# The low half of q and the second copy of k: written by the engines instead of by transfers

## The chip, the cores and the metric

One Trainium2 chip, one core. The time is that of one execution of the whole program on the device, in microseconds (us). The kernel before took 744.98 us, the median of 3 runs (744.69 to 747.67).

## The reference

One layer of a decoder on a sequence of 512 tokens with 1024 channels, in float32:

```
mod = silu(c) @ ada_w + ada_b          # shift1, scale1, gate1, shift2, scale2, gate2
h = rmsnorm(x) * (1 + scale1) + shift1
qa, ka, va, qb, kb, vb, ga, gb = split(h @ w_in)
ya = swa_attention(qa, ka, va) @ w_branch_a     # 8 query heads, 2 key heads, window of 128, sinks
yb = moba_attention(qb, kb, vb) @ w_branch_b    # 8 heads, blocks of 256
x = x + gate1 * ((sigmoid(ga) * ya + sigmoid(gb) * yb) @ w_out)
h2 = rmsnorm(x) * (1 + scale2) + shift2
x = x + gate2 * (relu(h2 @ w_mlp_in)^2 @ w_mlp_out)
out = rmsnorm(x)
```

A head is 64 wide, and the scores of both attentions are q times k with a bias by distance. With 512 tokens the second attention has two blocks, so that every query sees all earlier blocks.

## The kernel before

**Numbers in two parts.** A float32 value is held as a high part (rounded by ScalarE's copy into the matmul's type) and a low part (VectorE: value minus high part). `split(hi, lo, src)` at L69 to L72 does both: L71 on ScalarE, L72 on VectorE. A product of matrices is then three matmuls, high by high, low by high and high by low (`mm3`, L76 to L78).

**Scores.** A head has 64 channels, and the array takes 128 rows. So q is stacked: its high part on 64 partitions and its low part on the other 64. Tile `both[g]` is that stack for head g of a pair; head 0 has its high part on partitions 0 to 63, head 1 on 64 to 127. For k there are two tiles: `high[g]` has the high part on both halves, `low[g]` has the low part on one half and zeros on the other. A score then takes two matmuls of 128 rows, L440 in the loop of `Head.__init__`. The products q and k come out of the projection in PSUM, one bank (128 x 512) for a pair of heads: `g0p` and `pkv` for the windowed attention (tiles `qa`, `ka`), `pqk` for the other (tiles `qk`).

**The two functions that stack.** `stack_q` (L219 to L226) splits each half of the bank: high to its half of `both[g]`, low to a scratch tile `lo` at the same partitions, then a DMA on SyncE's queue takes `lo` to the other half (L225). `lo` has the tag `t`, a ring of three buffers that also gives `vaf` (L404), `ca*` and `cb*` (L483) and `sg*` (L573). `stack_k` (L228 to L235) splits into `high` and `low` and copies the high part to the other half by a DMA (L234). Callers: L401 and L406 (`qa0` to `qa3`), L403 (`ka`), L552 (`qk0` to `qk3`, q and k).

**Heads and dense work.** After the projections for the windowed attention (up to 58 us of the trace, with 0 to 58 in an order written by hand), `run` (L601) goes over 16 heads, 8 windowed (`a0`, `a4`, `a1`, ...) and 8 of the other attention (`b0` to `b7`). For each head in turn: scores (PSUM banks `sa*`, `sb*`; L440), on VectorE the bias and the row maximum (L441, into `pa*`, `pb*` and `ma*`, `mb*`), its negative (L444), on ScalarE the exponential (L445), the reciprocal of the sum (L451), the scaling (L456 on VectorE, L454 on ScalarE for block 3), transposes on TensorE (L470, banks `ta*`, `tb*`), a split of them (`pta*`, `ptb*`), the product with v (L481, banks `oa*`, `ob*`), a copy of the bank on ScalarE (L484, `ca*`, `cb*`) and one more matmul with a permutation, called swap here (L488), that adds the two halves; the result is split into `at0*`, `at1*`.

Between these steps `advance` takes steps of dense work from one list: the projection of v (`pv*`, weights `vw*` from the load `vbr*`, L511), of q and k (`pqk*`, weights `qkw*`), the gates (`pg*`, weights `gw*` from the load `gr*`, L566; sigmoid on ScalarE to `sg*`, L574), the branch products (`py*`, weights `bw*`), and the modulation for the second half (`ac2*`: ScalarE L154, VectorE L156, from the load `a`). The table `PACE` says how many steps stand at which place.

**What sets the order.** The program's order of every engine is fixed when the kernel is built. In the first stage and in the last ones it is written by hand; in between a scheduler places each engine's instructions by its own model of when operands and buffers are ready. Each engine then runs its list strictly in that order. PSUM has eight banks in one ring, and a bank that VectorE reads isn't read by ScalarE at the same time.

Of the kernel before, what the change touches and what calls it, by code (L numbers as in the profile page):

```python
# [10 lines left out]
F32 = mybir.dt.float32  # L11
F32R = mybir.dt.float32r
AF = mybir.ActivationFunctionType
ALU = mybir.AluOpType

P = 128
D = 1024
S = 512
# [19 lines left out]
def decoder_layer(ctx: ExitStack, tc: tile.TileContext, x, c, ada_w, ada_b, norm1_g, norm2_g, w_in,  # L38
# [3 lines left out]
    V, A, G, SY = nc.vector, nc.scalar, nc.gpsimd, nc.sync  # L42

    pz = ctx.enter_context(tc.tile_pool(name="pz", bufs=1, side="right"))
    p0 = ctx.enter_context(tc.tile_pool(name="p0", bufs=1))
# [23 lines left out]
    def split(hi, lo, src):  # L69

        A.activation(hi, src, AF.Copy)  # L71
        V.tensor_tensor(lo, src, hi.bitcast(F32), op=ALU.subtract)  # L72
# [38 lines left out]
    def slot(n, name, dt=F32):  # L111

        return p0.tile([P, 512], dt, name=name, tag=f"slot{n}")
# [96 lines left out]
    with ExitStack() as sa:  # L210
# [7 lines left out]

        def stack_q(name, src, both):  # L219

            lo = p0.tile([P, S], F32R, name=name + "l", tag="t", bufs=3)
            for g in range(2):
                r, o = slice(64 * g, 64 * g + 64), slice(64 - 64 * g, 128 - 64 * g)
                split(both[g][r], lo[r], src[r])
                SY.dma_start(both[g][o].bitcast(F32), lo[r].bitcast(F32))  # L225
            return both  # L226

        def stack_k(name, src, high, low):  # L228

            for g in range(2):  # L230
                r, o = slice(64 * g, 64 * g + 64), slice(64 - 64 * g, 128 - 64 * g)
                G.memset(low[g][o].bitcast(F32), 0.0)
                split(high[g][r], low[g][r], src[r])
                SY.dma_start(high[g][o].bitcast(F32), high[g][r].bitcast(F32))  # L234
            return high, low  # L235

        va = pa.tile([P, NT, 4, HD], F32R, name="va")
# [3 lines left out]
        with ExitStack() as ss:  # L241
# [152 lines left out]
            for s in range(2):  # L394
                w = wide(f"kvw{s}")
                split(w[0], w[1], kvr[:, :, s * P:(s + 1) * P])
                pkv.append(bank(f"pkv{s}"))
                for k in range(KT):
                    mm3(pkv[s], at(w, slice(None), k), at(hT, slice(None), k), first=k == 0, last=k == KT - 1)
                if s == 0:  # L400
                    qa = [stack_q("qa0", g0p[0], [qk_tile(f"qa0{g}") for g in range(2)])]  # L401
                    ka = [slot(n, f"ka{n}", F32R) for n in (4, 5, 6, 7)]
                    ka = stack_k("ka", pkv[0], ka[:2], ka[2:])  # L403
            vaf = scratch("vaf")  # L404
            A.activation(vaf, pkv[1], AF.Copy)
            qa += [stack_q(f"qa{j}", g0p[j], [qk_tile(f"qa{j}{g}") for g in range(2)]) for j in range(1, 4)]  # L406

        def turn_v():
# [126 lines left out]
        def proj_qk(i2):  # L535
            wr = []
            for s, col in ((0, C_QB), (1, C_KB)):
                t = raw(f"qkr{i2}{s}").rearrange("p (k n) -> p k n", k=KT)
                SY.dma_start(t, w0[:, :, col + i2 * 256:col + i2 * 256 + 256])
                wr.append(t)  # L540
            for half in range(2):
                i = 2 * i2 + half
                got, tiles = [], qk_tiles(f"qk{i}")
                for s in range(2):
                    w = cols_of(wr[s], half, f"qkw{i}{s}")
                    pb = bank(f"pqk{i}{s}")
                    for k in range(KT):
                        mm3(pb, at(w, slice(None), k), at(hT, slice(None), k), first=k == 0, last=k == KT - 1)
                        if k == 3:
                            yield  # L550
                    own = [[t[n] for t in tiles] for n in range(3)]
                    got.append(stack_q(f"qk{i}{s}", pb, own[0]) if s == 0 else stack_k(f"qk{i}{s}", pb, *own[1:]))  # L552
                    if s == 1:
                        qk[i] = got
                    yield
# [239 lines left out]
    for ci, (f0, f1) in enumerate(CHUNKS):  # L795
# [35 lines left out]
        else:  # L831
# [15 lines left out]
            for t in range(NT):  # L847
                o = [slot(4 + 2 * (t % 2) + h, f"o{t}{h}") for h in range(2)]
# [75 lines left out]
```

## Time and profile before

| | |
|---|---|
| median of 3 runs | 744.98 us |
| the profiled execution | 745.23 us |
| its span, first to last instruction | 743.5 us |
| mean granted clock of TensorE | 0.997 |
| busy TensorE, VectorE, ScalarE | 709.7, 459.1, 344.6 us |
| TensorE busy 58 to 240 us | 174.52 of 182 us |
| TensorE busy 300 to 700 us | 399.61 of 400 us |

TensorE works nearly all the time, so that what matters is where it stands still. The last two lines say that in the stage of the heads (58 to 240 us) it does so for 7.5 us, and in the long stage behind it hardly at all. Matmuls overlap in the profile: one of 128x512 is listed with 0.39 us while the next starts 0.23 us later, so that starts are read, not durations.

### The profile page before, as it was taken

How to read it: one execution, taken by the hardware profiler on the slowest of the kernel's cores; microseconds unless marked ns; L12 is line 12 of the kernel's file. 1: busy time of each engine (PE TensorE's matmuls, PEld its weight loads, DVE VectorE, ACT ScalarE, POOL GpSimd, SP SyncE). 2: the span in 40 equal slices, each digit the busy share in tenths (PEclk: the TensorE clock that was granted, in tenths of full speed). 3: DMA queues.
4: the chain of work that ended last, by engine and by line, in shares of the span. 5: the costliest groups of instructions: out<-in, count | busy, mean ns of one | idle time of the engine just before them, and what ended most of it. 6: DMA issues, size and time to landing. Idle time of an engine off the chain costs nothing.

```text
span 743.5 us, 9326 instructions
## 1 busy us (share of the span) xinstructions
PE 709.7 (95%) x3458; PEld 595.6 (80%) x3458; DVE 459.1 (62%) x959; ACT 344.6 (46%) x639; POOL 28.7 (4%) x40
## 2 busy tenths in 40 slices
PE   2799999998999999999999999999999999999996
PEld 1677889886887888888889888888888888888885
DVE  4874888887677867684478573252652527325765
ACT  3454787766786753343274442231332314322434
POOL 2220000000000000000120000000000000000001
PEclk9999999999999999999999999999999999999999
DMA  8994451566363864641415352233322332315103
GB/s 300 303 286 104 111 156 38 157 180 190 95 162 100 266 217 169 199 171 56 142 57 167 116 170 94 76 114 114 113 91 80 87 108 90 113 60 167 57 1 113
DMA packets 91146, 100.21 MB, mean 135 GB/s; under 512 B 3027, under 2 KB 70683, under 8 KB 91100
## 3 DMA queue, kind: packets, MB, share of 16 engines
q1 hardware_dynamic: 91100, 99.61, 43.6%
q8 instruction: 27, 0.44, 0.3%
q14 instruction: 19, 0.16, 0.1%
HBM read 94.03 MB, written 2.16 MB: 129 GB/s over the span
## 4 chain that ended last, share of the span: by engine, by line
PE 84%; ACT 4%; DMA 4%; DVE 3%; SPq 2%; issue 1%; POOL 0%; POOLq 0%; ACTq 0%; DVEq 0%
PE ph L77 8%; PE ph L76 8%; PE ph L78 8%; PE mo L78 7%; PE mo L76 7%; PE mo L77 7%; PE pg L76 3%; PE pg L78 3%; PE pg L77 3%; PE pqk L76 2%; PE py L78 2%; PE pqk L77 2%; PE py L76 2%; PE pqk L78 2%; PE py L77 2%
## 5 line engine op out<-in xcount | busy, mean ns | idle before, releaser
L800 ACT ACTIVATE r<-ph 128x512 f32<-128x512 f32 x32 | 18.8, 587 | 41.5 <-PE ph L78 26.8
L803 DVE TENSOR_TENSOR r<-r 128x512 f32<-128x512 f32 x32 | 21.9, 689 | 18.2 <-ACT a1h L802 8.0
L156 DVE SCALAR_TENSOR_TENSOR ac<-a,cs,ac 128x256 f32<-128x256 f32 x56 | 26.8, 479 | 3.5 <-ACT ac L154 2.9
L294 DVE SCALAR_TENSOR_TENSOR pac<-ad,cs,pac 128x256 f32<-128x256 f32 (+1 forms) x42 | 21.5, 523 | 9.8 <-ACT pac L292 9.4
L126 POOL TENSOR_TENSOR rstd<-rstd,mhalf 128x1 f32<-128x1 f32 x12 | 7.3, 610 | 373.3 <-DVE rstd L125 373.3
L711 DVE TENSOR_TENSOR rs<-mo,g2row 128x512 f32<-128x512 f32 x24 | 16.0, 686 | 9.1 <-PE mo L78 9.1
L445 ACT ACTIVATE pb<-pb,nb 128x128 f32<-128x128 f32 (+3 forms) x32 | 17.8, 557 | 8.1 <-DVE nb L444 7.7
L186 DVE SCALAR_TENSOR_TENSOR ma<-mw,cs,ma 128x512 f32<-128x512 f32 x28 | 21.0, 750 | 0.5
L76 PE MATMUL g0p<-hTh,g0h 128*128 128x512 f32 (+1 forms) x36 | 16.1, 448 | 3.8 <-ACT hTh L71 3.8
L445 ACT ACTIVATE pa<-pa,na 128x256 f32<-128x256 f32 (+1 forms) x32 | 15.2, 478 | 2.5 <-DVE na L444 2.4
L712 DVE TENSOR_TENSOR x_sb<-x_sb,rs 128x512 f32<-128x512 f32 x24 | 16.2, 685 | 0.0
L441 DVE CUSTOM_DVE_ANT_0 pa<-sa,ts,sink 128x256 f32<-128x256 f32 (+1 forms) x32 | 13.3, 445 | 3.8 <-PE sa L440 3.7
L441 DVE CUSTOM_DVE_ANT_0 pb<-sb,tm 128x128 f32<-128x128 f32 (+3 forms) x32 | 15.1, 488 | 0.2 <-PE sb L440 0.2
L77 PE MATMUL g0p<-hTl,g0h 128*128 128x512 f32 (+1 forms) x36 | 14.6, 406 | 0.0
L78 PE MATMUL g0p<-hTh,g0l 128*128 128x512 f32 (+1 forms) x36 | 14.4, 399 | 0.0
L440 PE MATMUL sb<-qk,qk 128*128 128x128 f32 (+3 forms) x64 | 12.8, 330 | 0.0
L76 PEld LDWEIGHTS g0p<-hTh,g0h 128*128 128x128 f32 x36 | 8.0, 222 | 5.1 <-ACT hTh L71 4.5
L282 POOL TENSOR_TENSOR g0l<-g0r,g0h 128x512 fp32r<-128x512 f32 x8 | 10.5, 1317 | 28.7 <-ACT g0h L281 24.4
L712 POOL TENSOR_TENSOR x_sb<-x_sb,rs 128x512 f32<-128x512 f32 x4 | 5.0, 1290 | 157.1 <-DVE rs L711 157.1
L440 PE MATMUL sa<-ka,qa 128*128 128x256 f32 (+1 forms) x64 | 10.9, 282 | 0.0
L470 PE MATMUL tb<-ident,pb 128*128 128x128 f32 x80 | 10.6, 274 | 0.3 <-DVE mb L441 0.3
L841 DVE TENSOR_TENSOR ml<-ml,g2row 128x512 f32<-128x512 f32 x8 | 5.1, 688 | 9.4 <-DMA ml<-in_w_mlp_out_dram 9.4
(1599 smaller groups left out, 2415.2 us busy)
## 6 DMA issues: line engine op xcount, KB each, us to landing
mi<-in_w_mlp_in_dram SPq DMA_DIRECT2D x16, 1024.0 KB, 6.3
mo<-in_w_mlp_out_dram SPq DMA_DIRECT2D x14, 1024.0 KB, 5.1
ad<-in_ada_w_dram SPq DMA_DIRECT2D x16, 512.0 KB, 7.9
a<-in_ada_w_dram SPq DMA_DIRECT2D x16, 512.0 KB, 5.3
gr<-in_w_in_dram SPq DMA_DIRECT2D x8, 1024.0 KB, 6.4
mw<-in_ada_w_dram SPq DMA_DIRECT2D x8, 1024.0 KB, 5.3
x_sb<-in_x_dram SPq DMA_DIRECT2D x8, 512.0 KB, 7.4
qkr<-in_w_in_dram SPq DMA_DIRECT2D x4, 1024.0 KB, 5.9
```

The lines of the kernel that those rows point to most:

```text
L76: nc.tensor.matmul(o, w[0], m[0], start=first, stop=False, **kw)
L77: nc.tensor.matmul(o, w[0], m[1], start=False, stop=False, **kw)
L78: nc.tensor.matmul(o, w[1], m[0], start=False, stop=last, **kw)
L156: V.scalar_tensor_tensor(acc, ad[:, k], cs[:, k:k + 1], acc, op0=ALU.mult, op1=ALU.add)
L186: V.scalar_tensor_tensor(acc, t[:, k], c1, acc, op0=ALU.mult, op1=ALU.add)
L294: V.scalar_tensor_tensor(part_ if k < KT - 1 else acc, ad(k), cs[:, k:k + 1], part_, op0=ALU.mult, op1=ALU.add)
L440: nc.tensor.matmul(pb[:, :w], q[g][:, i * P:e], k[n][g][:, e - w:e], start=n == 0, stop=n == 1)
L441: V.tensor_tensor_reduce(p[:, o:o + w], pb[:, :w], b[:, w - 1::-1] if w < b.shape[1] else b[:, ::-1], scale=SCALE, scalar=-3e38 if sk is N ...
L445: A.activation(p[:, o:o + w], p[:, o:o + w], AF.Exp, bias=neg[:, i:i + 1], accum_out=sums[:, i:i + 1])
L712: add.tensor_tensor(x_sb[:, t, cc], x_sb[:, t, cc], tm, op=ALU.add)
L800: A.activation(r, ph, AF.Relu)
L803: V.tensor_mul(r, r, r)
```

## The change

VectorE writes the low part of q straight to the other half of `both[g]`; the scratch tile `lo` and its DMA are gone. For k the second copy of the high part is made by ScalarE with one more copy out of PSUM, where a DMA took it from the first copy. 26 DMAs (16 of L225, 10 of L234) are no longer there, and 10 ScalarE instructions of 64x512 are new. From L226 on, the numbers of lines are lower by two in the kernel after.

```diff
         def stack_q(name, src, both):
 
-            lo = p0.tile([P, S], F32R, name=name + "l", tag="t", bufs=3)
             for g in range(2):
                 r, o = slice(64 * g, 64 * g + 64), slice(64 - 64 * g, 128 - 64 * g)
-                split(both[g][r], lo[r], src[r])
-                SY.dma_start(both[g][o].bitcast(F32), lo[r].bitcast(F32))
+                split(both[g][r], both[g][o], src[r])
             return both
 
         def stack_k(name, src, high, low):
...
                 G.memset(low[g][o].bitcast(F32), 0.0)
                 split(high[g][r], low[g][r], src[r])
-                SY.dma_start(high[g][o].bitcast(F32), high[g][r].bitcast(F32))
+                A.activation(high[g][o], src[r], AF.Copy)
             return high, low
```

The scheduler places the instructions of the stage of the heads anew. Up to 58 us and from about 245 us on the orders of all engines are the same as before. Three places follow; a name's last number is that of its buffer.

The first place is in front of head a0's scaling (near 81 us of the trace). VectorE before:

```order
L72 TENSOR_TENSOR qa3l_622<-g0p3_199,qa30_620 64x512
L441 ISA pa0_736,ma0_737<-sa02_752,ts0_734,sink_92 128x256
L441 ISA ma0_737 128x1
L72 TENSOR_TENSOR vw03l_773<-vbr0_641,vw03h_772 128x512
L444 TENSOR_SCALAR na0_739<-ma0_737 128x1 x2
L72 TENSOR_TENSOR va_91<-pva_727,va_91 128x4x128
L444 TENSOR_SCALAR na0_739<-ma0_737 128x1
L72 TENSOR_TENSOR qa3l_622<-g0p3_199,qa31_621 64x512
L441 ISA pa0_736,ma0_737<-sa03_758,ts0_734,sink_92 128x256
```

VectorE after:

```order
L72 TENSOR_TENSOR vw03l_761<-vbr0_629,vw03h_760 128x512
L439 ISA pa0_724,ma0_725<-sa01_734,ts0_722,sink_92 128x256
L439 ISA ma0_725 128x1
L442 TENSOR_SCALAR na0_727<-ma0_725 128x1
L439 ISA pa0_724,ma0_725<-sa02_740,ts0_722,sink_92 128x256
L439 ISA ma0_725 128x1
L72 TENSOR_TENSOR va_91<-pva_715,va_91 128x4x128
L439 ISA pa0_724,ma0_725<-sa03_746,ts0_722,sink_92 128x256
```

Both subtractions of `qa3` have moved ahead of these rows, and `vw03l` ahead of the scores `sa01` to `sa03`. ScalarE at the same place, before:

```order
L449 ACTIVATE ea0_764<-na0_739,sink_92 128x4
L71 ACTIVATE vb_634<-pv00_639 128x2x2x64
L445 ACTIVATE pa4_810,ua4_812<-pa4_810,na4_813 128x128
L445 ACTIVATE pa4_810,ua4_812<-pa4_810,na4_813 128x256 x2
L71 ACTIVATE vb_634<-pv01_640 128x2x2x64
L71 ACTIVATE vw10h_1305<-vbr1_1303 128x512
L71 ACTIVATE vw11h_1385<-vbr1_1303 128x512
L454 ACTIVATE pa0_736<-pa0_736,ua0_738 128x256
```

ScalarE after:

```order
L447 ACTIVATE ea0_752<-na0_727,sink_92 128x4
L443 ACTIVATE pa4_798,ua4_800<-pa4_798,na4_801 128x128
L71 ACTIVATE vw10h_1287<-vbr1_1285 128x512
L71 ACTIVATE vb_622<-pv00_627 128x2x2x64
L452 ACTIVATE pa0_724<-pa0_724,ua0_726 128x256
L71 ACTIVATE vb_622<-pv01_628 128x2x2x64
L71 ACTIVATE vw11h_1367<-vbr1_1285 128x512
```

`vw10h`, the high part of a weight of the load `vbr1`, has moved ahead of the copy to `vb` and, with fewer instructions between, stays ahead of head a0's scaling (L454, now L452).

The second place is at the scores of head a7 (near 137 us). VectorE before:

```order
L441 ISA pa7_1471,ma7_1472<-sa70_1475,ts7_1469,sink_92 128x128
L441 ISA ma7_1472 128x1
L156 SCALAR_TENSOR_TENSOR ac20_1593<-a20_1590,cs_86,ac20_1593 128x256
L444 TENSOR_SCALAR na7_1474<-ma7_1472 128x1
L441 ISA pa7_1471,ma7_1472<-sa71_1481,ts7_1469,sink_92 128x256
```

VectorE after:

```order
L439 ISA pa7_1453,ma7_1454<-sa71_1463,ts7_1451,sink_92 128x256
L439 ISA ma7_1454 128x1
L439 ISA pa7_1453,ma7_1454<-sa72_1469,ts7_1451,sink_92 128x256
L439 ISA ma7_1454 128x1
L442 TENSOR_SCALAR na7_1456<-ma7_1454 128x1
L72 TENSOR_TENSOR vb_622<-pv10_1283,vb_622 128x2x128
L439 ISA pa7_1453,ma7_1454<-sa73_1475,ts7_1451,sink_92 128x256
L439 ISA ma7_1454 128x1
L442 TENSOR_SCALAR na7_1456<-ma7_1454 128x1
L156 SCALAR_TENSOR_TENSOR ac20_1575<-a20_1572,cs_86,ac20_1575 128x256
```

The first step of `ac20` has moved from in front of the score `sa71` to behind the score `sa73`.

The third place is at the end of head b0 and the first gate (near 177 us). ScalarE before:

```order
L71 ACTIVATE gw02h_2136<-gr02_2134 128x1024
L71 ACTIVATE qk211_1571<-pqk21_1689 64x512
L71 ACTIVATE qk300_1735<-pqk30_1745 64x512
L71 ACTIVATE ptb10h_1994<-tb10_1993 128x512
L71 ACTIVATE ptb11h_2003<-tb11_2002 128x512
L484 ACTIVATE cb0_1904<-ob0_1895 128x512
L574 ACT_TABLE_LOAD
L574 ACTIVATE sg00_1987<-pg00_1912 128x512
```

ScalarE after:

```order
L482 ACTIVATE cb0_1880<-ob0_1871 128x512
L154 ACTIVATE ac22_1910<-a22_1907,cs_86 128x256
L443 ACTIVATE pb2_1915,ub2_1917<-pb2_1915,nb2_1918 128x128
L443 ACTIVATE pb2_1915,ub2_1917<-pb2_1915,nb2_1918 128x256
L71 ACTIVATE gw02h_2112<-gr02_2110 128x1024
L572 ACT_TABLE_LOAD
L572 ACTIVATE sg00_1963<-pg00_1888 128x512
L71 ACTIVATE at1h_625<-ob0_1871 64x512
L71 ACTIVATE qk211_1553<-pqk21_1668 64x512
L71 ACTIVATE qk300_1714<-pqk30_1724 64x512
L71 ACTIVATE ptb10h_1970<-tb10_1969 128x512
L71 ACTIVATE ptb11h_1979<-tb11_1978 128x512
```

`cb0` has moved ahead of `gw02h`, and the two `qk` copies and the two of `ptb1` from ahead of `sg00` to behind it. On TensorE the swap with `cb0` has moved ahead of the last score of head b2 and of b1's ten transposes.

## Rows read from the trace of the kernel before

**Rows 1.** The page's first part: busy time of each engine, share of the span and instructions.

```profile
PE 709.7 (95%) x3458; PEld 595.6 (80%) x3458; DVE 459.1 (62%) x959; ACT 344.6 (46%) x639; POOL 28.7 (4%) x40
```

**Rows 2.** The list of waits of TensorE (PE) between 55 and 240 us: waiting tile and line, released by; us in total, times, longest.

```profile
PE ob L488 <- ACT cb L484: 2.0, 1, 2.0
PE ob L481 <- ACT ptb40h L71: 1.7, 1, 1.7
PE pg L76 <- ACT sg L574: 1.4, 1, 1.4
PE ta L470 <- DVE pa L456: 1.2, 1, 1.2
...
PE pqk L76 <- DVE ma L441: 0.6, 1, 0.6
```

**Rows 3.** Busy time of each engine in stretches: stretch and its length, PE, PEld, DVE, ACT, POOL (instructions), granted clock, share of the DMA engines, GB/s.

```profile
58.00:240.00 182.00, 174.52 (x995) 151.81 (x994) 135.28 (x399) 128.33 (x277) 4.16 (x8) 0.99 0.49 132
80.00:90.00 10.00, 8.76 (x61) 7.83 (x60) 8.46 (x35) 9.14 (x28) 0.52 (x1) 1.00 0.61 160
180.00:190.00 10.00, 7.78 (x26) 6.10 (x27) 4.79 (x11) 6.99 (x13) 0.00 (x0) 0.83 0.63 154
230.00:240.00 10.00, 8.31 (x39) 6.62 (x38) 6.95 (x15) 8.78 (x17) 0.00 (x0) 1.00 0.28 71
300.00:700.00 400.00, 399.61 (x1824) 332.99 (x1824) 211.18 (x308) 140.79 (x223) 7.63 (x8) 1.00 0.35 113
```

**Rows 4.** The removed DMAs, from the views of lines L225 and L234: issue time in ns (min/median/max), first and last start; then the time to landing. The last line is of the waits of SyncE's queue between 58 and 250 us.

```profile
L225 SPq DMA_DIRECT2D qk<-qk30l x2: 467/1322/2176, 181.5 to 199.0; - x2
...
DMA to landing us min/median/max: 2.2/4.2/6.8
...
L234 SPq DMA_DIRECT2D qk<-qk x8: 461/467/511, 105.0 to 213.6; - x8
...
DMA to landing us min/median/max: 2.2/2.5/4.9
...
SPq L234 <- ACT qk L71: 20.4, 5, 6.8
```

**Rows 5.** Groups of ScalarE's (ACT) instructions between 58 and 240 us, by shape: count, busy us, mean ns, and the idle time just before them with its releaser.

```profile
L71 ACT ACTIVATE qk<-pqk 64x512 fp32r<-64x512 f32 x16 | 9.5, 591 | 1.0 <-PE sb L440 0.4 <-PE sa L440 0.3
...
L71 ACT ACTIVATE ka<-pkv 64x512 fp32r<-64x512 f32 x2 | 1.2, 584 | 1.5 <-DVE ka L72 1.5
```

**Rows 6.** VectorE (DVE) in order of time around the subtractions of `qa2`: start and duration in us. The first `qa2l` is on partitions 0 to 63, the second on 64 to 127.

```profile
75.89 0.68 DVE L72 TENSOR_TENSOR qa2l<-g0p,qa 64x512 fp32r<-64x512 f32 x1
76.50 0.67 DVE L72 TENSOR_TENSOR vw02l<-vbr,vw02h 128x512 fp32r<-128x512 f32 x1
77.23 0.69 DVE L72 TENSOR_TENSOR qa2l<-g0p,qa 64x512 fp32r<-64x512 f32 x1
77.96 0.35 DVE L441 CUSTOM_DVE_ANT_0 pa<-sa,ts,sink 128x128 f32<-128x128 f32 x1
```

**Rows 7.** Around head a0's transposes: TensorE and VectorE in order of time (start, duration, and in brackets the idle time before), then the landing of the two loads `vbr` of L511.

```profile
84.51 0.40 PE L440 MATMUL sa<-ka,qa 128*128 128x256 f32 x2
86.15 0.96 PE L470 MATMUL ta<-ident,pa 128*128 128x128 f32 x5 [1.24 <-DVE pa L456]
...
79.64 0.68 DVE L72 TENSOR_TENSOR vw03l<-vbr,vw03h 128x512 fp32r<-128x512 f32 x1
...
81.14 0.69 DVE L72 TENSOR_TENSOR qa3l<-g0p,qa 64x512 fp32r<-64x512 f32 x1
81.86 0.48 DVE L441 CUSTOM_DVE_ANT_0 pa<-sa,ts,sink 128x256 f32<-128x256 f32 x1
...
DMA to landing us min/median/max: 5.9/7.7/9.6
```

**Rows 8.** Around 137 us: TensorE, ScalarE and VectorE in order of time, as in rows 7.

```profile
138.74 0.50 PE L76 MATMUL pqk<-hTh,qkw20h 128*128 128x512 f32 x1 [0.64 <-DVE ma L441]
...
136.00 0.51 ACT L154 ACTIVATE ac<-a,cs 128x256 f32<-128x256 f32 x1 [3.00 <-DMA a<-in_ada_w_dram]
...
136.54 0.48 DVE L156 SCALAR_TENSOR_TENSOR ac<-a,cs,ac 128x256 f32<-128x256 f32 x1 [1.95 <-ACT ac L154]
```

**Rows 9.** From 177 to 183 us: TensorE, then ScalarE, in order of time, as in rows 7.

```profile
178.42 0.44 PE L470 MATMUL tb<-ident,pb 128*128 128x128 f32 x2 [0.33 <-DVE mb L441]
180.81 0.51 PE L488 MATMUL ob<-cb,swap 128*128 128x512 f32 x1 [1.96 <-ACT cb L484]
182.72 0.80 PE L76 MATMUL pg<-hTh,gw01h 128*128 128x512 f32 x1 [1.40 <-ACT sg L574]
...
177.02 1.06 ACT L71 ACTIVATE gw02h<-gr 128x1024 fp32r<-128x1024 f32 x1 [1.39 <-PE sb L440]
...
180.17 0.59 ACT L484 ACTIVATE cb<-ob 128x512 fp32r<-128x512 f32 x1
180.78 1.28 ACT L574 ACT_TABLE_LOAD   x1
182.07 0.60 ACT L574 ACTIVATE sg<-pg 128x512 f32<-128x512 f32 x1
```

**Rows 10.** Around 237 us: TensorE in order of time, as in rows 7, then, from the view of line L566, the wait of ScalarE's `gw06h` for its load (us in total, times).

```profile
237.31 0.50 PE L481 MATMUL ob<-ptb40h,vb 128*128 128x512 f32 x1 [1.69 <-ACT ptb40h L71]
...
  ACT gw06h L71: 3.2, 1
```

## The prediction

> **What bounds the kernel now.** I read the page first: TensorE is busy 95% of the span, VectorE 62%, ScalarE 46% [rows 1]. So an edit that takes work from the DMA queue and gives ScalarE ten instructions can only pay where TensorE stands still. The last removed transfer is issued at 213.6 us [rows 4]. From 300 to 700 us TensorE is busy 399.61 of 400 us, but from 58 to 240 us only 174.52 of 182 [rows 3]; the 7.5 us between these are what can be won there, with one thing more: in 180 to 190 us the granted clock was 0.83.
>
> Next, the list of TensorE's waits in that stretch [rows 2]. No line of it names a DMA of L225 or L234. They are waits of 0.6 to 2.0 us for ScalarE (L484, L71, L574) and VectorE (L456, L441), one each. Whoever reads only the removed DMAs must therefore say "hidden": they take 2.2 to 6.8 us to land [rows 4], and nothing on TensorE waits for that. The one large wait that they cause is SyncE's own queue, 20.4 us for ScalarE's `qk` [rows 4], which costs TensorE nothing by itself.
>
> What remains is the order. ScalarE and VectorE take their work strictly as the program's order lists it, and the change rewrites that order between 58 and 240 us (the rows under the diff). The reason stands in the code: `lo` came out of the same three-buffer ring `t` as `c*`, `sg*` and `vaf`, and `both` and `high` were complete only after a landing. Without these the planner puts `c*`, `sg*` and the scores elsewhere. So I take each place where TensorE waits and ask whether the instruction that it waited for now comes earlier.
>
> **Removed.** 26 DMAs of 128 KB, at about 0.47 us of SyncE's issue time each, one stretched to 2.18 [rows 4]. On TensorE's path: nothing, since none is waited for. Later DMAs on SyncE's queue no longer stand behind L234's wait for ScalarE; that is worth something only where a load is waited for (place 4).
>
> **Added.** Ten ScalarE copies of 64x512 out of PSUM. The nearest row is the first copy of the same bank, `qk<-pqk`, 591 ns [rows 5]: 10 x 0.59 = 5.9 us. ScalarE has 182 - 128.33 = 53.7 us idle in this stretch [rows 3], so the sum is covered if they fall into it. But a copy can't read while VectorE reads that bank: the second `ka` copy waited 1.53 us for VectorE's `ka` [rows 5]. A chain per half is now ScalarE 0.59, VectorE 0.69, ScalarE 0.59, and whatever stands behind the third waits too. Ends: 0 (all covered) and 10 x (0.59 + 0.69) = 12.8 us. I take 0 here, because in the order the copies mostly stand some places behind their VectorE subtraction, and put the places where I see them delay TensorE below.
>
> The Trainium skill speaks against this part of the change: "PSUM — Partial Sum Buffer", section "PSUM bank collisions raise a hardware error", says that two engines must not touch one bank and quadrant at once, two readers included, so that a third reader adds a link to a chain. The 1.53 us of [rows 5] agree. By the rule all ten links would count, and the sum below would be -5.2 + 12.8 = +7.6, or 752.6 us; by the trace, whose ScalarE has the idle time, few do.
>
> **Changed in place.** VectorE's 16 subtractions keep their shape, 0.69 us; only the output half moves. No row of before shows an output on the other half. Nearest: a subtraction on the lower half is overlapped by the next instruction (75.89 + 0.68 = 76.57, the next starts at 76.50), one on the upper half isn't (77.23 + 0.69 = 77.92, next at 77.96) [rows 6]. Difference 0.11 us. If each of the eight lower-half ones now loses its overlap on both sides, that is 16 x 0.11 = 1.8 us of VectorE, out of 182 - 135.28 = 46.7 us idle. I take 0 on the path, with 1.8 as the end of the range.
>
> The Trainium skill ("VectorE: DVE Perf Modes", section "Two Vector instructions with no wait between them") has this as a rule: an instruction whose output starts in another quadrant than the last one waits until all before it are done. It gives the same 1.8 us and no more.
>
> **Moved: four places, by TensorE's waits.**
>
> Place 1, 84.5 us. Head a0's transposes could have started at 84.75 (two score matmuls from 84.51, 0.12 apart) and start at 86.15, waiting for the scaling at L456 [rows 7]. VectorE had subtracted `qa3l` at 81.14 and only then took the last score `sa03` at 81.86. Now both `qa3l` are ahead of the score's row and a0's scaling stands right after its scores. I get the scaling done at 83.0 to 83.8, so the 1.4 us go; I take -1.3. What speaks against it: `vw10h`, which needs the load `vbr1`, now stands ahead of a0's last scaling on ScalarE. The load is issued when `vw03l` is done, at 79.64 + 0.68 = 80.3; I estimate 78.8 for it now, since two `qa3l` and one `sa` no longer stand between, and with the shorter landing of 5.9 us the data are there at 84.7. With 7.7 to 9.6 us [rows 7] the wait comes back as 1 to 1.5 us.
>
> Place 2, 137 us. `pqk` waits 0.64 us for VectorE's `ma`, and starts at 138.74. VectorE had sat 1.95 us until `ac20`, because ScalarE waited 3.00 us for the load `a` [rows 8], and `sa71` to `sa73` stood behind that L156. Now all four scores stand ahead of it. I take the 0.64 and the refill around it together: -0.9.
>
> Place 3, 178 to 186 us. Transposes at 178.42, then `ob<-cb` at 180.81 (1.96 waited for `cb`), then `pg` at 182.72 (1.40 waited for `sg`) [rows 9]. ScalarE had four copies between `gw02h` (177.02) and `cb` (180.17), then loads the sigmoid's table (1.28), then `sg` at 182.07. Now `cb0` stands ahead of `gw02h`, and `gw02h`, table and `sg00` follow without these four. `gw02h` still starts when TensorE lets it: 177.02 + 1.06 + 1.28 + 0.60 = 180.0, so `pg01` starts at 180.05: 182.72 - 180.05 = -2.7. With it goes the clock. 0.83 over 10 us is 3.4 us at 1.2 instead of 2.4 GHz; half of that, 1.7 us, is lost work. Before that, TensorE had waited 1.96 and 1.40 us one right behind the other. Single waits of 1.24 us (place 1) and 1.69 (place 4) left the clock of 80 to 90 and of 230 to 240 us at 1.00 [rows 3]. What remains here is one wait of about 1.2 us. I take -1.6.
>
> Place 4, 235 us. `ob<-ptb40h` waits 1.69 us [rows 10]; ScalarE was late since it waited 3.2 us for the load of `gw06h`. That load goes out about 1 us earlier, but `gw06h` now stands ahead of `cb3` and `sg04`, so the wait appears at an earlier matmul. I take +0.2 for both.
>
> New waits. `ca4` now stands behind `qkw11h`, an `at0h` and a `qk` copy, about 1.06 + 2 x 0.59 = 2.2 us: between 0 and 2.2; +0.6, since ScalarE has room there. Head b1's `cb1` is wanted earlier on TensorE and has an added copy ahead: between 0 and 1.3; +0.5.
>
> **Sum.** -1.3 - 0.9 - 2.7 - 1.6 + 0.2 + 0.6 + 0.5 = -5.2 us. The profiled execution took 745.23 us (span 743.5); the median is 744.98, 0.25 lower. 744.98 - 5.2 = 739.8.
>
> **Rivals.** 0.5% is 3.7 us, about what a measurement of this kernel can tell from no change.
>
> (A) The forecast, 739.8, between 735.5 and 741.2. The lower end: all 7.5 us of idle time and the 1.7 of the clock go, 744.98 - 9.2 = 735.8. Chance 0.50.
>
> (B) No change. The transfers were hidden, and the new order has its own waits. For it: TensorE's list names none of them [rows 2]. If place 3 holds only half (its 4.3 us become 2.1), `vbr1` gives 1.3 back, and the copies cost three links of 0.59, then -5.2 + 2.2 + 1.3 + 1.8 = +0.1: 745. Span of this case 741.3 to 748.7. Chance 0.37.
>
> (C) Slower: ScalarE becomes what TensorE waits for. Each copy waits for its subtraction (0.69) and then takes 0.59, with exponentials, `c*` and `sg*` queued behind it. Against the other gains it decides from (5.2 + 3.7) / 1.28 = 7 of the ten links on the path; at eight, -5.2 + 10.2 gives 750. Against it: the 53.7 us of idle time. Chance 0.10.
>
> (D) The change doesn't do what it says: a write into the other half is slow. At twice 0.69 the 16 cost 11 us of VectorE; half of it hidden by 46.7 us idle leaves +5.5, which eats the gain: 745. Chance 0.03.
>
> **Range and chances.** Faster 0.50 (A), same 0.40 (B, D), slower 0.10 (C). The range 735.5 to 745.5 holds A and the nearer half and more of B; outside are C and the far part of B.
>
> **What would show it.** `pg` of place 3 starting at most 1.3 us behind the last transposes, and no 10 us with a clock under 0.95: place 3 right. No wait of `ta` for L456 near 85 us: place 1; a wait for `vw10h` instead: the load. No `pqk` wait for `ma`: place 2. The new copies at 0.59 us and the subtractions at 0.69: prices right. TensorE's waits for ScalarE lines together above 8 us would be case C; a list of the same total with other names, case B. The forecast is wrong if the sum of idle time between 58 and 240 us does not fall by 3 us or more.

## The result and the profile after

The kernel after took 743.24 us, the median of 20 runs (739.35 to 745.56); the kernel before, run as often beside it, 746.01 us (744.69 to 749.48; the first three of these runs are the ones shown ahead of the prediction). The ratio is 0.9947 with an interval of 0.9933 to 0.9960: 4.0 us faster, between 3.0 and 5.0. The time lies in the range of the prediction. The forecast of -5.2 us was a good microsecond too large, and it stood on the 744.98 us of three runs, a microsecond under the 746.01 of twenty.

The profiled execution has a span of 740.5 us, 3.0 less than before. TensorE's waits in the same stretch, 55 to 240 us (the list that answers to [rows 2]; lines are two lower):

```profile
PE ob L486 <- ACT cb L482: 1.9, 1, 1.9
PE tb L468 <- ACT sg L572: 1.3, 1, 1.3
PE pg L76 <- ACT sg L572: 1.1, 1, 1.1
PE pkv L76 <- ACT kvw0h L71: 0.4, 1, 0.4
PE ta L468 <- DVE pa L454: 0.2, 1, 0.2
```

Of the five waits of [rows 2], the 1.7 us for `ptb40h`, the 1.2 us for head a0's scaling and the 0.6 us for `ma` are gone. That for `cb` is still 1.9 us long, but it is another `cb`, 44 us later. The stretches of [rows 3] show the same (length, PE, PEld, DVE, ACT, POOL, granted clock, DMA share, GB/s):

```profile
58.00:240.00 182.00, 177.39 (x1009) 154.54 (x1009) 138.21 (x404) 136.46 (x289) 4.19 (x8) 0.98 0.43 122
80.00:90.00 10.00, 10.00 (x67) 9.07 (x66) 6.88 (x26) 7.48 (x25) 0.00 (x0) 1.00 0.34 111
130.00:140.00 10.00, 10.00 (x67) 9.17 (x66) 7.54 (x25) 6.71 (x20) 0.00 (x0) 1.00 0.50 129
180.00:190.00 10.00, 10.00 (x52) 8.56 (x52) 6.35 (x21) 9.62 (x17) 0.52 (x1) 1.00 0.61 176
220.00:230.00 10.00, 7.01 (x27) 5.21 (x26) 4.45 (x11) 7.18 (x13) 0.00 (x0) 0.73 0.13 42
230.00:240.00 10.00, 10.00 (x49) 8.49 (x48) 6.25 (x15) 6.72 (x13) 0.00 (x0) 0.93 0.77 211
```

Places 1 and 2 are whole: 10.00 of 10 us in 80 to 90 and 130 to 140 us. 180 to 190 us is whole too, but place 3 has moved ahead of it, to 173 to 177 us; the clock is at 1.00 in all. The hole is now in 220 to 230 us, with a clock of 0.73. TensorE's idle time from 58 to 240 us fell from 182 - 174.52 = 7.5 us to 182 - 177.39 = 4.6.

Place 3 in order of time, TensorE and then ScalarE (start, duration, idle time before):

```profile
174.25 1.04 PE L468 MATMUL tb<-ident,pb 128*128 128x128 f32 x8
176.58 0.44 PE L468 MATMUL tb<-ident,pb 128*128 128x128 f32 x2 [1.29 <-ACT sg L572]
176.77 0.48 PE L76 MATMUL pg<-hTh,gw01h 128*128 128x512 f32 x1
...
173.55 1.06 ACT L71 ACTIVATE gw02h<-gr 128x1024 fp32r<-128x1024 f32 x1 [1.05 <-DMA gr<-in_w_in_dram]
174.63 1.28 ACT L572 ACT_TABLE_LOAD   x1
175.93 0.60 ACT L572 ACTIVATE sg<-pg 128x512 f32<-128x512 f32 x1
```

`gw02h`, table and `sg00` stand one behind the other, as the prediction read from the order; one wait of 1.29 us is left where [rows 9] had 1.96 and 1.40, and the clock stays.

Place 4, TensorE, ScalarE and SyncE's queue:

```profile
221.35 1.15 PE L468 MATMUL tb<-ident,pb 128*128 128x128 f32 x9
224.35 0.55 PE L486 MATMUL ob<-cb,swap 128*128 128x512 f32 x1 [1.85 <-ACT cb L482]
224.71 0.41 PE L468 MATMUL tb<-ident,pb 128*128 128x128 f32 x1
226.26 0.79 PE L76 MATMUL pg<-hTh,gw05h 128*128 128x512 f32 x1 [1.14 <-ACT sg L572]
...
231.53 0.40 PE L76 MATMUL pg<-hTh,gw05h 128*128 128x512 f32 x1
...
217.07 0.51 ACT L154 ACTIVATE ac<-a,cs 128x256 f32<-128x256 f32 x1 [1.16 <-PE pm L163]
222.76 1.06 ACT L71 ACTIVATE gw06h<-gr 128x1024 fp32r<-128x1024 f32 x1 [5.18 <-DMA gr<-in_w_in_dram]
223.72 0.58 ACT L482 ACTIVATE cb<-ob 128x512 fp32r<-128x512 f32 x1
224.32 1.28 ACT L572 ACT_TABLE_LOAD   x1
225.61 0.60 ACT L572 ACTIVATE sg<-pg 128x512 f32<-128x512 f32 x1
...
215.86 0.37 SPq L564 DMA_DIRECT2D gr<-in_w_in_dram  x1
```

ScalarE sits 5.18 us in front of `gw06h`, whose load went out at 215.86. `cb3`, the table and `sg04` need nothing of that load but are queued behind it, and TensorE waits for both. This is place 3 of before over again, the fall of the clock included: from 226.26 to 231.53 twelve starts take 5.27 us, where 0.23 each would be 2.8.

The prices of the new instructions, ScalarE and VectorE by shape, 58 to 240 us (count, busy, mean ns, idle before):

```profile
L71 ACT ACTIVATE qk<-pqk 64x512 fp32r<-64x512 f32 x16 | 9.4, 588 | 0.2
...
L232 ACT ACTIVATE qk<-pqk 64x512 fp32r<-64x512 f32 x8 | 4.8, 594 | 2.6 <-DVE qk L72 2.4
...
L72 DVE TENSOR_TENSOR qa<-g0p,qa 64x512 fp32r<-64x512 f32 x8 | 5.5, 689 | 6.2 <-ACT qa L71 6.0
```

### The profile page after: what moved, and what is told of

Read it like the earlier page. It is cut to its first block, busy times and chain, and to the rows that moved or that the text cites. A ratio compares the mean times of both kernels' runs of the same rounds, so it can differ in the third digit from the quotient of the medians.

```text
span 740.5 us, 9260 instructions
## 1 busy us (share of the span) xinstructions
PE 710.7 (96%) x3458; PEld 595.5 (80%) x3458; DVE 460.7 (62%) x959; ACT 351.0 (47%) x649; POOL 28.8 (4%) x40
## 2 busy tenths in 40 slices
DMA packets 89065, 96.79 MB, mean 131 GB/s; under 512 B 2611, under 2 KB 70267, under 8 KB 89020
## 4 chain that ended last, share of the span: by engine, by line
PE 81%; DMA 6%; ACT 5%; DVE 4%; SPq 2%; issue 2%; POOLq 0%; POOL 0%; ACTq 0%; DVEq 0%
PE ph L77 8%; PE ph L78 8%; PE ph L76 8%; PE mo L77 7%; PE mo L78 7%; PE mo L76 7%; PE pg L76 4%; PE pg L77 3%; PE pg L78 3%; DMA ad<-in_ada_w_dram 3%; PE py L77 2%; PE py L76 2%; PE py L78 2%; DMA gr<-in_w_in_dram 2%; PE pqk L76 2%
## 5 line engine op out<-in xcount | busy, mean ns | idle before, releaser
L297 PEld LDWEIGHTS pac<-ones_r,acc 128*128 128x128 f32 x32 | 5.5, 242 | 7.9 <-DVE acc L292 4.4
L72 DVE TENSOR_TENSOR qk<-pqk,qk 64x512 fp32r<-64x512 f32 x16 | 11.0, 688 | 1.1 <-ACT qk L71 0.7
L297 PE MATMUL pac<-ones_r,acc 128*128 128x1 f32 x32 | 5.4, 278 | 6.3 <-DVE rstd L125 4.2
```

## The experiments

The theory: neither the removed transfers nor the added copies change the time by themselves; the order of ScalarE's and VectorE's queues does, at four places, and the scheduler turned it over because the ring `t` was no longer held. The rivals: the transfers' traffic and SyncE's queue; the copies' time on ScalarE.

Each kernel was timed beside the kernel before; the column us is the ratio's distance from 1 times the median of the kernel before in the same series (746.0 to 748.1). The stage in the last column is read from one trace each, from the first matmul of `pkv` with `kvw1h` to the first matmul of `ph`. What lies behind it takes 358.1 to 359.1 us in all ten traces. What lies ahead of it takes 56.3 to 59.1 us, though every engine's order is the same there: chance, so that spans of single traces are not compared. By the same chance five of the traces, `q_only`, `gw06_behind_sg04`, `copies_twice`, `both_edges` and `q_only_both_edges`, begin the stage at the lower clock. Of 57 to 62 us, before and then `q_only`:

```profile
57.00:62.00 5.00, 4.79 (x29) 3.94 (x28) 2.93 (x3) 1.81 (x3) 0.11 (x1) 1.00 0.23 57
57.00:62.00 5.00, 4.80 (x23) 4.24 (x23) 2.74 (x3) 1.63 (x3) 0.00 (x0) 0.66 0.30 74
```

A clock of 0.66 over 5 us is 3.4 us at 1.2 instead of 2.4 GHz, so that half of that, up to 1.7 us, is in the stages of these five and not in the others. The column us, from many runs, decides.

| kernel | ratio to before | interval | us | stage |
|---|---|---|---|---|
| before | 1 | | 0 | 327.7 |
| after | 0.9947 | 0.9933 to 0.9960 | -4.0 | 325.4 |
| q_only | 0.9884 | 0.9851 to 0.9916 | -8.7 | 320.6 |
| k_only | 1.0017 | 1.0000 to 1.0035 | +1.3 | 329.1 |
| gw06_behind_sg04 | 0.9890 | 0.9863 to 0.9917 | -8.2 | 321.0 |
| copies_twice | 0.9961 | 0.9941 to 0.9981 | -2.9 | 326.1 |
| ring_held | 0.9988 | 0.9967 to 1.0008 | -0.9 | 327.6 |
| transfers_back | 0.9947 | 0.9928 to 0.9966 | -4.0 | 324.3 |
| both_edges | 0.9883 | 0.9856 to 0.9910 | -8.7 | 319.6 |
| q_only_both_edges | 0.9854 | 0.9825 to 0.9884 | -10.9 | 318.7 |

**One half of the change at a time.** `q_only` is the kernel before with the first hunk of the diff, `k_only` with the second.

> Only stack_q is changed; stack_k keeps its ten DMAs. Theory (the order of the queues decides): the rows of places 1, 2 and 3 stand as in the kernel after, and gw06h stands ahead of cb3 and sg04 as there, so the time is that of the kernel after, about 4 us under before (2.5 to 5.5). Rival, the transfers' own traffic: 16 of 26 are gone, so about 2.4 us under before. Rival, ScalarE's ten copies cost their 5.9 us: without them about 9.9 us under before.

> Only stack_k is changed; stack_q keeps lo, its ring and its 16 DMAs. Theory: lo holds the ring t, so cb0 and sg00 stay behind the copies at place 3 and that place costs what it cost before; place 2 is gone (-1); gw06h stands ahead of cb3 and sg04, which costs 3.5 to 4 us: in all about 2.5 us slower than before (0 to 4). Rival, traffic: 10 of 26 transfers gone, 1.5 us faster. Rival, the copies cost 5.9 us: 5.9 us slower, with waits of TensorE for the copies' line.

`k_only` came out as the theory has it: `cb0` and `sg00` stand where they stood before, and TensorE waits at place 3 and at place 4. The first two lines of its list of waits, 55 to 245 us:

```profile
PE ob L488 <- ACT cb L484: 3.5, 2, 1.9
PE pg L76 <- ACT sg L574: 2.5, 2, 1.4
```

`q_only` did not: -8.7 where the theory said -4 and the rival of the copies -9.9. In its trace places 1 to 3 are as in the kernel after; the difference is place 4. Its queue of SyncE and ScalarE there:

```profile
214.18 0.37 SPq L564 DMA_DIRECT2D gr<-in_w_in_dram  x1
...
219.68 1.06 ACT L71 ACTIVATE gw06h<-gr 128x1024 fp32r<-128x1024 f32 x1 [3.58 <-DMA gr<-in_w_in_dram]
...
221.04 0.58 ACT L482 ACTIVATE cb<-ob 128x512 fp32r<-128x512 f32 x1
```

The same row stands ahead of `cb3`, but its load goes out 2.5 us earlier (214.18 against 215.86, counted from stages that begin at 57.45 and 56.65) and lands 1.4 us faster (219.68 - 214.18 = 5.5 against 222.76 - 215.86 = 6.9). On SyncE's queue it waits 3.3 us for VectorE's `ub`, in the kernel after 6.2 us for VectorE's `ptb32l`, so the order sets this too. `cb3` is done before TensorE asks for it, and the clock of 220 to 240 us stays at 1.00. So the price of place 4 hangs on when a load lands, and my expectation had taken it for fixed. By its time alone the rival of the copies would fit as well; the next run and `copies_twice`, below, decide against it.

**Place 4 alone.** One edge of order in the kernel after:

```diff
+            sig = {}
...
-                    w = cols_of(wr, n % 2, f"gw{s}{n}")
+                    with tc.issue_after(sig[4]) if (s, n) == (0, 6) else nullcontext():
+                        w = cols_of(wr, n % 2, f"gw{s}{n}")
...
-                    A.activation(sg, pg, AF.Sigmoid)
+                    sig[n] = A.activation(sg, pg, AF.Sigmoid).ins
```

> The kernel after with one edge of order: the split of gw06 is queued behind the sigmoid sg04 on ScalarE. Theory: the waits for cb3 (1.9) and sg04 (1.1) near 224 us and the stretch at the lower clock behind them (5 us at half speed, 2.4 us lost) go: about 5 us under the kernel after, 9 under before (6.5 to 10.5). Rival, the load of gr06 is late for TensorE in any order: the wait comes back at ptb40h or pg06, and the time stays at 4 us under before.

4.2 us under the kernel after (8.2 - 4.0); the stage is 4.3 us shorter. Both waits of place 4 have gone from TensorE's list, and nothing has come in their place:

```profile
PE tb L468 <- ACT sg L574: 1.1, 1, 1.1
PE ta L468 <- DVE pa L454: 0.4, 2, 0.2
```

This shows the cause of place 4: the row of `gw06h` stands ahead of `cb3` and `sg04` while its load is late. The load came no earlier here (issued 160.6 us into the stage, 159.2 in the kernel after), and ScalarE still waits 2.53 us for it, but with nothing behind it that TensorE needs at once. `q_only` left the row and had the load earlier; either is enough. And with all ten copies this kernel is about as fast as `q_only` without them (8.2 and 8.7), which speaks against the copies' time.

**The ring.** In the kernel after, GpSimd fills a tile of the ring `t` and a DMA reads it:

```diff
+            lo = p0.tile([P, S], F32, name=name + "l", tag="t", bufs=3)
...
                 split(both[g][r], both[g][o], src[r])
+                G.tensor_copy(lo[r], both[g][r].bitcast(F32))
+                SY.dma_start(spare[r], lo[r])
...
+        spare = dr.tile([P, S], F32, name="spare")
```

> The kernel after, and for each stacked half of q GpSimd copies the high part into a tile of the ring t, which a DMA on SyncE's queue then takes to a spare tensor that nobody reads: the ring is held as lo held it, and 16 of the 26 transfers are back. Theory: cb0 and sg00 move back behind the copies, so place 3 costs again what it cost before (about 4.5 us more than in the kernel after), places 1 and 2 keep their gain, place 4 its loss: 0 to 3 us over before, like k_only. Rival, the ring is not the reason and only the transfers' place in front of the scores counted: the time stays 4 us under before.

-0.9 us, with 0 in its interval, against -4.0 without the held ring; that is just under the expected 0 to 3. The stage is back at 327.6. The order of ScalarE at place 3 is that of the kernel before, `cb0` and `sg00` behind four copies, and so are the waits there:

```profile
178.38 0.51 PE L490 MATMUL ob<-cb,swap 128*128 128x512 f32 x1 [1.48 <-ACT cb L486]
180.29 0.79 PE L76 MATMUL pg<-hTh,gw01h 128*128 128x512 f32 x1 [1.40 <-ACT sg L576]
```

The held ring thus brings place 3 back, with q still written straight to its half; `k_only`, where `lo` itself holds the ring, has place 3 as before too. (What the 16 copies on GpSimd do apart from the ring no run shows.) Places 1 and 2 keep their gain here: the waits for `pa` (1.2) and `ma` of [rows 2] don't come back, so those two don't come from the ring. They are gone in `q_only` and in `k_only` as well, so either half of the change is enough for them; that the shorter chain to the scores is the reason is likely, and not tested apart.

**The transfers.** In the kernel after, 26 DMAs of the removed size to a tensor that nobody reads:

```diff
                 split(both[g][r], both[g][o], src[r])
+                SY.dma_start(spare[r], both[g][o].bitcast(F32))
...
                 A.activation(high[g][o], src[r], AF.Copy)
+                SY.dma_start(spare[r], high[g][r].bitcast(F32))
...
+        spare = dr.tile([P, S], F32, name="spare")
```

> The kernel after, plus 26 DMAs of the removed size on SyncE's queue, from the stacked tiles to a spare tensor in HBM that nobody reads. The orders of TensorE, VectorE and ScalarE are those of the kernel after. Theory: the transfers were hidden, so about 4 us under before (2 to 5.5). Rival, queue and traffic: they delay the loads gr06 and vbr1 behind them, and the time goes back to that of before or above.

-4.0, as without them. The page has 100.21 MB again, like the kernel before (96.79 after). The orders are those of the kernel after but for some instructions between 84 and 100 us, where TensorE waits for nothing in either. The rival of traffic and queue falls.

**The copies.** Each of the ten is made twice.

> The kernel after with each of ScalarE's ten second copies of k made twice (20 instead of 10). Theory: ScalarE has room, so only the changed order counts: 1 to 5 us under before. In its order ac20 stands between the scores of head a7 again (+1). Rival, the copies lie on TensorE's path at 0.59 us each and up to 1.28 with their chain: 5.9 to 12.8 us over the kernel after, 2 to 9 us over before.

-2.9: 1.0 us over the kernel after, for ten more copies of 0.59 us, and the intervals overlap. A part of it is order. TensorE's list names no copy; it has the wait for `ma` of place 2 back at 0.8 us, where `ac20` stands between the scores again. The rival of the copies' time falls.

**Both edges.** `gw02` behind `sg00` and `gw06` behind `sg04`, in the kernel after and in `q_only`.

> The kernel after with gw02 queued behind sg00 and gw06 behind sg04. Theory: what was left at place 3 (1.1 us of waiting for sg00) goes as well: about 1.2 us under gw06_behind_sg04, 9.4 under before (8 to 11). Rival: the later gw02 delays pg02 by as much, and it stays at 8.

> Only stack_q changed, with both edges of order. Theory: q_only without its waits of 1.1 us (sg00) and 0.4 us (sg04): about 10.3 us under before (9 to 12), the fastest of all. Rival: as q_only, 8.7 under before.

The fastest is the change of q alone with both edges, 736.11 us in the median where the kernel before took 748.08. TensorE has no idle time left in the stretch of [rows 3] (the clock of 0.99 is that of its first 2 us):

```profile
58.00:240.00 182.00, 182.00 (x1046) 159.82 (x1045) 144.11 (x429) 134.09 (x293) 4.30 (x8) 0.99 0.47 132
```

`both_edges` gained 0.5 us on `gw06_behind_sg04` in the ratio and 1.4 in the stage, where 1.2 was expected; its 0.3 us wait of `py` for a second copy of k (L232) is the one place in any of these traces where TensorE waits for such a copy. That the change of k costs 1 to 2 us once place 4 is mended (stages 319.6 and 318.7, -8.7 and -10.9 us) is likely and not settled: the intervals overlap.

## Why the prediction was right, and where its sum was off

**Removed, 0 us.** Right, by `transfers_back`.

**Added, 0 us with 12.8 as the end.** Right at 0.59 us each, by [rows 5] and the trace after. ScalarE waited 2.4 us for VectorE's `qk` in front of two of the copies, so the chain that the prediction names is there; TensorE waited for none of them, and `copies_twice` costs 1.0 us, not 5.9 to 12.8. The rule of the Trainium skill ("PSUM — Partial Sum Buffer", section "PSUM bank collisions raise a hardware error") says why the copy has to wait; that all ten links would count is not borne out.

**Changed in place, 0 us with 1.8 as the end.** Right: 689 ns now, where [rows 6] had 0.68 and 0.69 us for writes to the same half.

**Place 1, -1.3 us.** Right: the wait is gone, 1.4 us. VectorE's scaling began at 82.03. The load went out at 77.59 and was there 5.5 us later, sooner than the 5.9 of the prediction's good case; even so `vw10h` waited 1.11 us for it, with head a0's last scaling, on ScalarE, behind it. But the five transposes at 83.76 read only what VectorE had scaled; the two that read the last one come at 87.28. So the price of this risk, 1 to 1.5 us, was read at the wrong transposes: in `transfers_back` `vw10h` waited 3.11 us, and TensorE not at all.

```profile
83.76 0.71 PE L468 MATMUL ta<-ident,pa 128*128 128x128 f32 x5
...
87.28 0.38 PE L468 MATMUL ta<-ident,pa 128*128 128x128 f32 x2
...
82.03 0.81 DVE L454 TENSOR_SCALAR pa<-pa,ua 128x128 f32<-128x128 f32 x3
...
83.08 0.63 ACT L71 ACTIVATE vw10h<-vbr 128x512 fp32r<-128x512 f32 x1 [1.11 <-DMA vbr<-in_w_in_dram]
...
83.88 0.50 ACT L452 ACTIVATE pa<-pa,ua 128x256 f32<-128x256 f32 x1
...
77.59 0.38 SPq L509 DMA_DIRECT2D vbr<-in_w_in_dram  x1
```

**Place 2, -0.9 us.** Right: gone. From the seven transposes to `pqk` TensorE loses nothing now:

```profile
134.28 0.93 PE L468 MATMUL ta<-ident,pa 128*128 128x128 f32 x7
134.96 0.48 PE L76 MATMUL pqk<-hTh,qkw20h 128*128 128x512 f32 x1
```

**Place 3, -2.7 and -1.6 for the clock.** Right: 1.3 us of waiting are left, no fall of the clock. Before, 178.42 to 182.72 was 4.3 us for two transposes and a swap, some 0.5 us of starts, and 1.7 us went to the clock: 5.5 lost. Now it is 1.4 (from the eighth transpose, about 175.2, to 176.58). That is 4.1 us, where 4.3 were forecast. The ring as its reason, which the prediction took from the code, is shown by `ring_held` and `k_only`.

**Place 4, +0.2 us.** This is the step that failed. The prediction saw that `gw06h` stands ahead of `cb3` and `sg04`, and put the wait "at an earlier matmul" at the price of the later one. It measured about +4 us: waits of 1.85 and 1.14, and 5.27 - 2.8 = 2.5 us lost to the clock, together 5.5, against 1.7 before [rows 10]. `gw06_behind_sg04` gives it back, 4.2 us. Two things were missed. ScalarE's row was priced by the one wait that it had caused, not by everything queued behind it: a copy, a table load of 1.28 us and a sigmoid, for which TensorE waits one after the other. And at place 3 the prediction had read from the trace that two waits right behind each other had gone with a fall of the clock, but did not ask whether place 4 now had the same pair.

**New waits, +0.6 and +0.5.** Neither came: `ca4` and `cb1` were in time. Only short waits appeared elsewhere, as the 0.2 us for `pa` in the list above. These 1.1 us offset a part of the missing 4, so that the sum was nearer than its terms, which is luck.

Of the rivals, (C) and (D) are excluded by the prices above. (B), no change, is excluded by the interval of the ratio, not by the time alone: 743.24 us lies in the span of 741.3 to 748.7 that the prediction gave to no change, and above 741.2, where (A) ends. On the forecast's own base the ratio makes 744.98 x 0.9947 = 741.0, just inside (A). The thought of (B) was half right: the gain of the first three places, about 6.5 us, was given back to more than half by a new wait, at a place that it did not name. The prediction's own mark, a fall of TensorE's idle time by 3 us or more, this one trace just misses (2.9), and its mark of no 10 us with a clock under 0.95 is missed in 220 to 240 us, at place 4. The single trace gained 2.4 us in the stage, about half of the forecast, the median of 20 runs 4.0; how far the clock falls at place 4 differs from trace to trace (0.73 and 0.93 here, 0.89 and 0.94 in the same two stretches of `transfers_back`).

## What to carry to other kernels

An edit that takes a tile out of a ring, or a transfer out of a chain, can move the work of every engine behind it when a scheduler sets the order: price the new order at each place where the bounding engine waits, not the edit. Of an instruction that waits for a load, ask what is queued behind it on its engine; everything there inherits the wait. The same row cost 4 us ahead of a copy and a sigmoid and nothing behind them. Half of a change may be worth more than the whole: here q alone is 8.7 us faster, the full change 4.0; with both edges of order it is 10.9 and 8.7, which the intervals do not tell apart.

## What the runs showed of the hardware

A write of 64x512 to the other half of the partitions costs what a write to the same half costs: 689 against 688 ns on VectorE, 594 against 588 on ScalarE. And TensorE's clock fell in the middle of a stage that was otherwise full, behind two waits 1.9 us apart: 1.96 and 1.40 us at place 3 before, 1.85 and 1.14 at place 4 after, with a matmul every 0.43 instead of 0.23 us from 226.85 to 231.12. The pairs at the same places in the other traces did the same, but for one: `ring_held` had 1.24 and 1.13 us at place 4, and the clock of 230 to 240 us stayed at 1.00. Single waits of 1.1 to 1.7 us inside the stage left it at 1.00. At the head of the stage, near 57 us, it fell in five traces, behind waits of 1.4 to 3.1 us for `kvw0h`, and stayed in two others behind 2.0 and 2.1 us (`transfers_back`, `ring_held`). So the length of a wait alone does not tell in these traces when it falls.
